# Layer normalisation without affine terms: separate rings for x and y, tiles of 8 rows, and a last store cut into 120 and 8 partitions

## Chip, cores, metric

The kernel runs on one core of one Trainium2 chip. The metric is device time in microseconds; lower is better. The time of a run is some 2 us longer than the span of its profile, which counts from the first to the last instruction.

## The reference

```python
def setup_inputs():
    return {"x": np.random.randn(32, 512, 1024).astype(np.float32), "eps": 1e-5}

def reference(x, eps):
    mean = np.mean(x, axis=-1, keepdims=True)
    var = np.var(x, axis=-1, keepdims=True)
    return ((x - mean) / np.sqrt(var + eps)).astype(np.float32)
```

That is 16384 rows of 1024 floats, 67.11 MB in and 67.11 MB out.

## The kernel before

It takes 4 rows on each of 128 partitions at a time (2 MB), with six buffers for x and six for y. Loads are issued from SP, stores from ACT.

```python
K = 4
xin = ctx.enter_context(tc.tile_pool(name="xin", bufs=6))
yout = ctx.enter_context(tc.tile_pool(name="yout", bufs=6))
st = ctx.enter_context(tc.tile_pool(name="st", bufs=4))
for t in range(ntiles):                                     # 32 tiles
    xt = xin.tile([P, K, D], fdt)
    nc.sync.dma_start(out=xt, in_=x2[rows].rearrange("(p k) d -> p k d", p=P))
    for k in range(K):                                      # DVE: 2 bn_stats and 1 bn_aggr a row
        ...
    # DVE: negmean, vpe = var + eps, ivar = 1 / vpe;  ACT: rstd = sqrt(ivar);  POOL: nmr = negmean * rstd
    ...
    yt = yout.tile([P, K, D], fdt)
    for k in range(K):
        nc.scalar.activation(out=yt[:, k, :], in_=xt[:, k, :], func=AF.Identity,
                             bias=nmr[:, k : k + 1], scale=rstd[:, k : k + 1])
    dst = o2[rows].rearrange("(p k) d -> p k d", p=P)
    nc.scalar.dma_start(out=dst, in_=yt)
```

Of the kernel before, what the change touches and what calls it, by code (L numbers as in the profile page):

```python
# [1 line left out]

# [4 lines left out]


@with_exitstack  # L10
def kernel(
    ctx: ExitStack,
    tc: tile.TileContext,
    x: bass.AP,
    eps: bass.AP,
    out: bass.AP,
):
    nc = tc.nc
    P = nc.NUM_PARTITIONS

    eps_val = float(eps) if not isinstance(eps, bass.AP) else 1e-5

    x2 = x.flatten_outer_dims()
    o2 = out.flatten_outer_dims()
    N, D = x2.shape
    BN_MAX = nc.vector.BN_STATS_FMAX
    assert D % BN_MAX == 0
    NSUB = D // BN_MAX

    K = 4  # L30
    rows_per_tile = P * K
    assert N % rows_per_tile == 0
    ntiles = N // rows_per_tile

    xin = ctx.enter_context(tc.tile_pool(name="xin", bufs=6))
    yout = ctx.enter_context(tc.tile_pool(name="yout", bufs=6))
    st = ctx.enter_context(tc.tile_pool(name="st", bufs=4))

    fdt = mybir.dt.float32
    AF = mybir.ActivationFunctionType  # L40
    ALU = mybir.AluOpType

    for t in range(ntiles):
        rows = slice(t * rows_per_tile, (t + 1) * rows_per_tile)

        xt = xin.tile([P, K, D], fdt)
        nc.sync.dma_start(out=xt, in_=x2[rows].rearrange("(p k) d -> p k d", p=P))  # L47

        stats = st.tile([P, K, NSUB, 6], fdt)
        mv = st.tile([P, K, 2], fdt)  # L50
        for k in range(K):
            for s in range(NSUB):
                nc.vector.bn_stats(  # L53
                    out=stats[:, k, s, :],
                    in_=xt[:, k, s * BN_MAX : (s + 1) * BN_MAX],
                )
            nc.vector.bn_aggr(out=mv[:, k, :], in_=stats[:, k, :, :])  # L57
        negmean = st.tile([P, K], fdt)
        nc.vector.tensor_scalar_mul(out=negmean, in0=mv[:, :, 0], scalar1=-1.0)  # L59
        vpe = st.tile([P, K], fdt)  # L60
        nc.vector.tensor_scalar(  # L61
            out=vpe, in0=mv[:, :, 1], scalar1=eps_val, scalar2=None, op0=ALU.add
        )
        ivar = st.tile([P, K], fdt)
        nc.vector.reciprocal(out=ivar, in_=vpe)  # L65

        rstd = st.tile([P, K], fdt)
        nc.scalar.activation(out=rstd, in_=ivar, func=AF.Sqrt, bias=0.0, scale=1.0)  # L68

        nmr = st.tile([P, K], fdt)  # L70
        nc.gpsimd.tensor_mul(out=nmr, in0=negmean, in1=rstd)  # L71

        yt = yout.tile([P, K, D], fdt)
        for k in range(K):
            nc.scalar.activation(  # L75
                out=yt[:, k, :],
                in_=xt[:, k, :],
                func=AF.Identity,
                bias=nmr[:, k : k + 1],
                scale=rstd[:, k : k + 1],  # L80
            )

        dst = o2[rows].rearrange("(p k) d -> p k d", p=P)
        nc.scalar.dma_start(out=dst, in_=yt)


# [1 line left out]
_INS = ['x', 'eps']  # L88
_OUTS = [((32, 512, 1024), 'float32')]
#: Inputs that are plain numbers.  # L90
_NUMBERS = {'eps': 1e-05}


# [26 lines left out]
```

## Time and profile before

| | before |
|---|---|
| time, median of 3 runs | 321.23 us (321.14 to 321.33) |
| span of the profiled run | 319.0 us |
| busy: DVE, ACT | 181.6 us, 154.3 us |
| bytes, mean rate | 134.27 MB, 421 GB/s |

The page of a profile gives each engine's busy time, then strips of 40 slices of the span. A digit is the busy share of a slice in tenths. In a table of windows each line has: start and end in us, length, the busy us of DVE, ACT and POOL (with their instructions), the clock, the busy share of the 16 DMA engines, and GB/s. A DMA packet is booked in the window in which it starts, so a narrow window can show a share above 1 (2.69 from 314.0 to 314.2 us of this kernel).

### The profile page before, as it was taken

Reading aid. Unit: us, or ns where it says so; the run is one execution under the profiler, and the core shown is the slowest. Engines: PE = TensorE matmul, PEld = TensorE weight load, DVE = VectorE, ACT = ScalarE, POOL = GpSimd, SP = SyncE. Lnnn points to the kernel's source line nnn. Section 1 sums busy time; section 2 is a strip of 40 time slices with the busy share of each in tenths; the row PEclk is TensorE's granted clock in tenths of the full one; section 3 lists DMA queues with packets and bytes.
Section 4 is the critical chain, followed back from the end, with each engine's and each line's share of the span. In section 5 each row is a group of like instructions: output and inputs, shape, how many; then the busy total and the mean of one; then the engine's idle time right before and its main releaser. Section 6 shows DMA issues by size and latency. Waiting matters only on the chain.

```text
span 319.0 us, 926 instructions
## 1 busy us (share of the span) xinstructions
DVE 181.6 (57%) x480; ACT 154.3 (48%) x161; POOL 6.6 (2%) x36
## 2 busy tenths in 40 slices
DVE  0999764457754477544676355765446744467610
ACT  1147491651907419074380833809247091470970
POOL 0000000000000000000000000000000000000000
DMA  7999999999999999999999999999999999999995
GB/s 294 427 405 422 438 431 431 431 429 431 426 429 432 435 431 431 429 427 431 431 433 435 430 431 427 427 431 427 435 438 430 428 431 427 431 427 427 421 427 220
DMA packets 9222, 134.27 MB, mean 421 GB/s; under 512 B 1024, under 2 KB 1024, under 8 KB 1024
## 3 DMA queue, kind: packets, MB, share of 16 engines
q1 hardware_dynamic: 4608, 67.11, 49.6%
q10 hardware_dynamic: 4608, 67.11, 49.2%
q14 instruction: 6, 0.05, 0.0%
HBM read 67.11 MB, written 67.11 MB: 421 GB/s over the span
## 4 chain that ended last, share of the span: by engine, by line
DMA 87%; DVE 4%; issue 3%; ACT 2%; SPq 1%; POOLq 0%; POOL 0%; DVEq 0%
DMA xt<-in_x_dram 87%; DVE stats L53 3%; ACT yt L75 1%; SPq L47 1%; DVE mv L57 0%; DVE ivar L65 0%; DVE negmean L59 0%; POOLq L115 0%; ACT rstd L68 0%; POOL nmr L71 0%; DVE vpe L61 0%; DVEq L65 0%; DVEq L59 0%
## 5 line engine op out<-in xcount | busy, mean ns | idle before, releaser
L53 DVE BATCH_NORM_STATS2 stats<-xt 128x6 f32<-128x512 f32 x256 | 159.4, 665 | 115.3 <-DMA xt<-in_x_dram 115.3
L75 ACT ACTIVATE yt<-xt,nmr,rstd 128x1024 f32<-128x1024 f32 x128 | 146.7, 1227 | 4.7 <-POOL nmr L71 4.5
L68 ACT ACTIVATE rstd<-ivar 128x4 f32<-128x4 f32 x32 | 6.6, 205 | 149.6 <-DVE ivar L65 149.0
L57 DVE BATCH_NORM_AGGREGATE mv<-stats 128x2 f32<-128x12 f32 x128 | 25.1, 196 | 1.1
L71 POOL TENSOR_TENSOR nmr<-negmean,rstd 128x4 f32<-128x4 f32 x32 | 6.3, 198 | 297.9 <-ACT rstd L68 297.9
L65 DVE RECIPROCAL ivar<-vpe 128x4 f32<-128x4 f32 x32 | 5.7, 178 | 3.0
L59 DVE TENSOR_SCALAR negmean<-mv 128x4 f32<-128x4 f32 x32 | 5.4, 170 | 3.1
L61 DVE TENSOR_SCALAR vpe<-mv 128x4 f32<-128x4 f32 x32 | 5.2, 162 | 0.0
L68 ACT ACT_TABLE_LOAD x1 | 1.3, 1283 | 0.7 <-PEq L101 0.7
L101 POOL MEMSET const-float32-0.0<- 128x1 f32 x1 | 0.1, 98 | 0.2 <-issue 0.2
L101 POOL MEMSET const-uint8-127<- 128x1 uint8 x1 | 0.1, 102 | 0.0
L101 POOL MEMSET const-bfloat16-1.0<- 128x1 bf16 x1 | 0.1, 101 | 0.0
L101 POOL MEMSET const-float32-1.0<- 128x1 f32 x1 | 0.1, 98 | 0.0
## 6 DMA issues: line engine op xcount, KB each, us to landing
xt<-in_x_dram SPq DMA_DIRECT2D x32, 2048.0 KB, 38.4
out_dram<-yt ACTq DMA_DIRECT2D x32, 2048.0 KB, 15.5
```

The source lines that it names most:

```text
L47: nc.sync.dma_start(out=xt, in_=x2[rows].rearrange("(p k) d -> p k d", p=P))
L53: nc.vector.bn_stats(out=stats[:, k, s, :], in_=xt[:, k, s * BN_MAX : (s + 1) * BN_MAX],)
L57: nc.vector.bn_aggr(out=mv[:, k, :], in_=stats[:, k, :, :])
L59: nc.vector.tensor_scalar_mul(out=negmean, in0=mv[:, :, 0], scalar1=-1.0)
L61: nc.vector.tensor_scalar(out=vpe, in0=mv[:, :, 1], scalar1=eps_val, scalar2=None, op0=ALU.add)
L65: nc.vector.reciprocal(out=ivar, in_=vpe)
L68: nc.scalar.activation(out=rstd, in_=ivar, func=AF.Sqrt, bias=0.0, scale=1.0)
L71: nc.gpsimd.tensor_mul(out=nmr, in0=negmean, in1=rstd)
L75: nc.scalar.activation(out=yt[:, k, :], in_=xt[:, k, :], func=AF.Identity, bias=nmr[:, k : k + 1], scale=rstd[:, k : k + 1],)
L101: nc = _bacc.Bacc("TRN2", target_bir_lowering=False, num_devices=1)
```

## The change

The intent: larger transfers with fewer packets, the same 48 rows a partition in two rings instead of twelve buffers, small tiles at the end so that little stands after the last load, and a last store that takes work off a DMA engine that is late. The statistics are shortened as well: eps becomes the bias of ACT's square root, and one fused DVE instruction takes the place of the POOL product.

```diff
+TILES = (8, 8, 8, 8, 8, 8, 8, 8, 8, 8, 8, 8, 8, 8, 8, 4, 2, 2)
+XRING = 32
+YRING = 16
+GROUP = 4
+def place(tiles, ring):      # position of each tile in a ring; starts over where a tile does not fit
+    ...
-    xin = ctx.enter_context(tc.tile_pool(name="xin", bufs=6))
-    yout = ctx.enter_context(tc.tile_pool(name="yout", bufs=6))
+    xr = rings.tile([P, XRING, D], fdt)
+    yr = rings.tile([P, YRING, D], fdt)
     ...
-        nc.vector.tensor_scalar_mul(out=negmean, ...)
-        nc.vector.tensor_scalar(out=vpe, ..., op0=ALU.add)
-        nc.vector.reciprocal(out=ivar, in_=vpe)
-        nc.scalar.activation(out=rstd, in_=ivar, func=AF.Sqrt, bias=0.0, scale=1.0)
-        nc.gpsimd.tensor_mul(out=nmr, in0=negmean, in1=rstd)
+        nc.scalar.activation(out=std[:, :G], in_=mv[:, :G, 1], func=AF.Sqrt, bias=eps_t, scale=1.0)
+        nc.vector.reciprocal(out=rstd[:, :G], in_=std[:, :G])
+        nc.vector.scalar_tensor_tensor(out=nmr[:, :G], in0=mv[:, :G, 0], scalar=-1.0,
+                                       in1=rstd[:, :G], op0=ALU.mult, op1=ALU.mult)
     ...
+    with tc.manual_schedule():
+        for (K, row, xp), (_, _, yp) in zip(place(TILES, XRING), place(TILES, YRING)):
+            nc.sync.dma_start(out=xr[:, xp : xp + K, :], in_=rows_of(x2, row, K))
+            for g in range(0, K, GROUP):
+                group(...)                       # statistics and normalisation of up to 4 rows
+            dst, src = rows_of(o2, row, K), yr[:, yp : yp + K, :]
+            cuts = ((0, 120), (120, P)) if (row + K) * P == N else ((0, P),)
+            for a, b in cuts:
+                nc.scalar.dma_start(out=dst[a:b], in_=src[a:b])
```

More of the change, by code (lines that the diff above doesn't have):

```diff
@@ L7 @@
 from concourse._compat import with_exitstack
+TILES = (8, 8, 8, 8, 8, 8, 8, 8, 8, 8, 8, 8, 8, 8, 8, 4, 2, 2)
[3 more added lines that the diff above has]
+def place(tiles, ring):
+    plan, row, pos = [], 0, 0
+    for K in tiles:
+        if pos + K > ring:
+            pos = 0
+        plan.append((K, row, pos))
+        row += K
+        pos += K
+    return plan
 @with_exitstack
@@ L26 @@
     BN_MAX = nc.vector.BN_STATS_FMAX
-    assert D % BN_MAX == 0
     NSUB = D // BN_MAX
-    K = 4
-    rows_per_tile = P * K
-    assert N % rows_per_tile == 0
-    ntiles = N // rows_per_tile
-    xin = ctx.enter_context(tc.tile_pool(name="xin", bufs=6))
-    yout = ctx.enter_context(tc.tile_pool(name="yout", bufs=6))
+    assert sum(TILES) * P == N
+    rings = ctx.enter_context(tc.tile_pool(name="rings", bufs=1))
     st = ctx.enter_context(tc.tile_pool(name="st", bufs=4))
@@ L41, with rows_of, group @@
     ALU = mybir.AluOpType
-    for t in range(ntiles):
-        rows = slice(t * rows_per_tile, (t + 1) * rows_per_tile)
-        xt = xin.tile([P, K, D], fdt)
-        nc.sync.dma_start(out=xt, in_=x2[rows].rearrange("(p k) d -> p k d", p=P))
-        stats = st.tile([P, K, NSUB, 6], fdt)
-        mv = st.tile([P, K, 2], fdt)
-        for k in range(K):
+    xr = rings.tile([P, XRING, D], fdt)
+    yr = rings.tile([P, YRING, D], fdt)
+    eps_t = rings.tile([P, 1], fdt)
+    def rows_of(a, row, K):
+        return a[row * P : (row + K) * P].rearrange("(p k) d -> p k d", p=P)
+    def group(xs, ys, G):
+        stats = st.tile([P, GROUP, NSUB, 6], fdt, name="stats")
+        mv = st.tile([P, GROUP, 2], fdt, name="mv")
+        for k in range(G):
             for s in range(NSUB):
@@ L54 @@
                     out=stats[:, k, s, :],
-                    in_=xt[:, k, s * BN_MAX : (s + 1) * BN_MAX],
+                    in_=xs[:, k, s * BN_MAX : (s + 1) * BN_MAX],
                 )
             nc.vector.bn_aggr(out=mv[:, k, :], in_=stats[:, k, :, :])
-        negmean = st.tile([P, K], fdt)
-        nc.vector.tensor_scalar_mul(out=negmean, in0=mv[:, :, 0], scalar1=-1.0)
-        vpe = st.tile([P, K], fdt)
-        nc.vector.tensor_scalar(
-            out=vpe, in0=mv[:, :, 1], scalar1=eps_val, scalar2=None, op0=ALU.add
-        )
-        ivar = st.tile([P, K], fdt)
-        nc.vector.reciprocal(out=ivar, in_=vpe)
-        rstd = st.tile([P, K], fdt)
-        nc.scalar.activation(out=rstd, in_=ivar, func=AF.Sqrt, bias=0.0, scale=1.0)
-        nmr = st.tile([P, K], fdt)
-        nc.gpsimd.tensor_mul(out=nmr, in0=negmean, in1=rstd)
-        yt = yout.tile([P, K, D], fdt)
-        for k in range(K):
+        std = st.tile([P, GROUP], fdt, name="std")
+        nc.scalar.activation(
+            out=std[:, :G], in_=mv[:, :G, 1], func=AF.Sqrt, bias=eps_t, scale=1.0
+        )
+        rstd = st.tile([P, GROUP], fdt, name="rstd")
+        nc.vector.reciprocal(out=rstd[:, :G], in_=std[:, :G])
+        nmr = st.tile([P, GROUP], fdt, name="nmr")
+        nc.vector.scalar_tensor_tensor(
+            out=nmr[:, :G],
+            in0=mv[:, :G, 0],
+            scalar=-1.0,
+            in1=rstd[:, :G],
+            op0=ALU.mult,
+            op1=ALU.mult,
+        )
+        for k in range(G):
             nc.scalar.activation(
-                out=yt[:, k, :],
-                in_=xt[:, k, :],
+                out=ys[:, k, :],
+                in_=xs[:, k, :],
                 func=AF.Identity,
@@ L81 @@
             )
-        dst = o2[rows].rearrange("(p k) d -> p k d", p=P)
-        nc.scalar.dma_start(out=dst, in_=yt)
+    with tc.manual_schedule():
+        nc.vector.memset(eps_t, eps_val)
+        for (K, row, xp), (_, _, yp) in zip(place(TILES, XRING), place(TILES, YRING)):
+            nc.sync.dma_start(out=xr[:, xp : xp + K, :], in_=rows_of(x2, row, K))
+            for g in range(0, K, GROUP):
+                G = min(GROUP, K - g)
+                a, b = xp + g, yp + g
+                group(xr[:, a : a + G, :], yr[:, b : b + G, :], G)
+            dst, src = rows_of(o2, row, K), yr[:, yp : yp + K, :]
+            cuts = ((0, 120), (120, P)) if (row + K) * P == N else ((0, P),)
+            for a, b in cuts:
+                nc.scalar.dma_start(out=dst[a:b], in_=src[a:b])
 _INS = ['x', 'eps']
```

## The prediction

> **What bounds the kernel now.** I read the page first (busy shares, then the 40 slices, then the queues), then the chain of waits, then windows over the whole span, then very short windows over its last microseconds.
>
> ```profile
> DVE 181.6 (57%) x480; ACT 154.3 (48%) x161; POOL 6.6 (2%) x36
> ...
> DMA  7999999999999999999999999999999999999995
> ...
> q1 hardware_dynamic: 4608, 67.11, 49.6%
> q10 hardware_dynamic: 4608, 67.11, 49.2%
> q14 instruction: 6, 0.05, 0.0%
> ...
> DMA 87%; DVE 4%; issue 3%; ACT 2%; SPq 1%; POOLq 0%; POOL 0%; DVEq 0%
> ```
>
> No compute engine is busy for even 60% of the span, while the DMA engines are at nine tenths or more in every slice but the first and the last. Loads (q1) and stores (q10) took equal shares of the engines for equal bytes. The chain is 87% load transfers. So the transfers are the bound: 67.11 MB in and 67.11 MB out, and the change touches neither figure.
>
> The windows (start:end, length, busy us per engine, clock, DMA share, GB/s) show how little is left:
>
> ```profile
> 0.00:2.00 2.00, 0.00 (x0) 1.27 (x1) 0.20 (x4) 1.00 0.39 74
> 2.00:4.00 2.00, 0.00 (x0) 0.01 (x1) 0.00 (x0) 1.00 0.70 213
> 4.00:14.00 10.00, 5.33 (x13) 0.00 (x0) 0.00 (x0) 1.00 1.01 434
> ...
> 40.00:290.00 250.00, 143.62 (x378) 123.97 (x129) 4.96 (x25) 1.00 1.01 431
> ...
> 315.60:319.00 3.40, 0.00 (x0) 0.00 (x0) 0.00 (x0) 1.00 0.03 14
> ```
>
> At 431 GB/s, 134.27 MB need 311.5 us. By 14 us 0.15 + 0.43 + 4.34 = 4.91 MB have moved, so the DMA behaves as if it had started at 14 - 4.91/0.431 = 2.6 us. The transfers nearly stop at 315.6 us, and 3.4 us of span follow. What is moving there is the finding that the change aims at:
>
> ```profile
> 315.40:315.60 0.20, 0.00 (x0) 0.00 (x0) 0.00 (x0) 1.00 0.19 82
> 315.60:315.80 0.20, 0.00 (x0) 0.00 (x0) 0.00 (x0) 1.00 0.00 0
> ...
> 316.00:316.20 0.20, 0.00 (x0) 0.00 (x0) 0.00 (x0) 1.00 0.19 82
> ...
> 316.60:316.80 0.20, 0.00 (x0) 0.00 (x0) 0.00 (x0) 1.00 0.19 82
> ...
> 317.20:317.40 0.20, 0.00 (x0) 0.00 (x0) 0.00 (x0) 1.00 0.19 82
> ```
>
> 82 GB/s for 0.2 us is 16.4 KB: one packet of 16 KB, one partition's share of a tile. They start 0.6 us apart, and 16 KB in 0.6 us is 27 GB/s, a sixteenth of 431. So a single DMA engine is finishing its partitions alone, until about 317.8 us, while the other fifteen were done near 315.4. The kernel ends some 2.4 us late for one engine.
>
> [...]
>
> **The change part by part.**
>
> *Statistics.* Out go the negated mean, the addition of eps and the POOL product (32 each); in come one fused DVE instruction and the reciprocal per group of up to 4 rows, 15 x 2 + 3 = 33 groups. DVE loses 32 x (170 + 162 + 178 ns) = 16.3 us of instructions and gains 33 x (178 + about 170) = 11.5; busy about 178 us. ACT stays near 154.5, POOL falls to its constants. None of it is on the path: 178 of 319 us is no bound.
>
> *Compute per tile.* A group's statistics take 5.3 us (42.97 to 48.28 in the chain). Sqrt (0.21), reciprocal (0.18), the fused product (0.17) and three handoffs of 0.05 to 0.08 add 0.75, then four normalisations take 4.63 on ACT beside the next group's statistics. A tile of 8 rows costs 2 x 6.05 = 12.1 us in steady state. Its transfers, 2 x 4.19 MB at 431, cost 19.5. Still DMA bound.
>
> *Buffers.* x has 32 rows against 24 now, y 16 against 24. The first store leaves after one load of 8 rows (2.6 + 9.7 + 1.1 = 13.4, the 1.1 being the first landing now, 8.60, minus 2.6 + 4.9), then two groups: 13.4 + 5.3 + 0.75 + 6.05 + 4.63 = 30.1 us, against 19.6 now. Meanwhile loads alone fill the engines; four tiles in the x ring last until 2.6 + 38.9 = 41.5 us, so nothing idles. The first store's bytes start near 32.5, as it must be issued (0.4) and get in behind queued loads (I allow 2). From then on the queues share equally, and loads keep a lead over stores of about (32.5 - 2.6) x 0.431 = 12.9 MB, 3.1 tiles, which fits the rings.
>
> *Packets.* If one partition's 8 rows move as one packet of 32 KB, there are half as many. [...] Semaphore packets per engine fall from 64 to about 37: 0.1 to 0.2 us.
>
> *Last store.* It is 1 MB: 64 KB per engine at 27 GB/s, 2.4 us. If the late engine is the last one, it gets none of it, and its 2.4 us of lateness are just paid off. [...] The extra DMA issue, 0.34 us on ACT, lies beside transfers.
>
> *Sum.* Fifteen engines: 315.4 - 1.1 + 0.3 = 314.6. The late one: 317.8 - 1.1 - 2.4 = 314.3. The end moves from 317.8 to 314.6, -3.2 us: 321.2 - 3.2 = 318.0 us.
>
> **The rivals.** *A hole near the end from the smaller y ring.* Tile 14 (8 rows) may be normalised only once store 12 has landed. From there: 4.63 + 0.75 + 4.63 = 10.1 us of compute, about 1.1 from issue to first byte (the first load's bytes come that long after its issue), and up to 2 for the late engine's part of store 12: 13.2 us. While loads still share the engines store 13 lasts 19.5 us and covers this; with the loads gone it lasts 9.7, and 3.5 us lie idle. With a lead of 3.1 tiles the loads would end just about when store 12 does, so this is a real danger. It would also let the late engine catch up, so the split would bring nothing: 315.4 + 3.5 - 1.1 + 0.3 = 318.1, +0.3: 321.5 us. What speaks against it: the last three loads, of 4, 2 and 2 rows, have packets of 16 and 8 KB beside store packets of up to 32 KB, and get, turn by turn, a third and then a fifth of the engines. 8 rows of loads then stretch from 19.5 us to about 14.6 + 24 = 39, during which stores move 8 + 16 rows, and the loads fill every hole. If packets stay at 16 KB, only the last 4 rows are slowed, and some 2 us of hole remain: about 320.
>
> *The late engine is not the last one, or lateness grows for another reason.* Then the split does nothing: only the 1.1 us of overhead go, 320.1.
>
> *The DVE-ACT round trip or the rings starve the DMA in the middle* (DVE waits for ACT's sqrt in every group, and ACT for a y slot). 12.1 of 19.5 us speaks against it; only a dependency tracked over whole rings would do it, and it would cost tens of us.
>
> *More than 2% faster* needs under 314.8. [...]
>
> **Range and chances.** I give the first sum 60% (318.0), the partly filled hole or the missed engine 25% (320), the full hole 12% (321.5), starvation 2 to 3%. The middle is 318.4; 8 in 10 lie within 316.8 to 321.3. The 2% lines are 314.8 and 327.7: faster 0.03, same 0.95, slower 0.02.
>
> **What would show it.** Right: the middle windows at 431 to 434 GB/s; about 5,200 DMA packets instead of 9,222; the last 15 us at full rate without an idle window; no train of lone 16.4 KB packets after the rest; ACT's first normalisation of a tile waiting for a landed store in the middle, harmlessly. Wrong: a window near 290 to 300 us with no bytes, with ACT waiting for an output transfer before it (the y ring); a lone late engine still there (the split missed); some 9,000 packets (no larger ones, no gain in rate); slices under 9 in the middle (starvation).

Its sum came to 318.0 us, 3.2 less than before:

- Packets, 1.1 us off for every engine. 1.0 of it was the estimate of what half as many packets are worth. The rest is for the semaphore packets: the records have 64 packets of 4 bytes per engine before and 36 after, of 9 ns each: 28 fewer are 0.25 us.
- Last store, 2.4 us off for the late engine and 0.3 on for others. The author took the part of 120 partitions to leave one engine out ("the last one" in the text), supposed that this is the late one, and took the part of 8 to give some of the others a ninth packet of 8 KB, 0.3 us. One engine left out and one with a ninth packet are in the records of the changed kernel (below). That the one left out is the late one they do not show: it ended at 312.1 us, the latest at 318.7.

The sum for "more than 2% faster": at the measured 431 GB/s it is 311.5 + 2.6 before the transfers + 1.2 after the last packet + 2.2 beyond the span, 317.5 us: still not under 314.8.

## The result

| | before | after |
|---|---|---|
| time, median of 4 runs | 321.28 us (321.14 to 321.36) | 321.80 us (321.31 to 323.10) |
| span of the profiled run | 319.0 us | 320.1 us |
| busy: DVE, ACT | 181.6, 154.3 us | 186.9, 158.1 us |
| DMA packets | 9222 | 5197 |

The ratio is 1.0023, with a 95% interval of 1.0003 to 1.0043: no gain, and a trace of a loss. (A ratio is the mean time of one kernel's fast runs over that of the other's of the same rounds, so it is not quite the ratio of the medians.) One of the four runs of the changed kernel, 323.10 us, stands apart from the other three. The main sum had forecast 3.2 us of gain; the medians show 0.5 us of loss.

From the page of the changed kernel, the strip, the rates and the queues:

```profile
DMA  8999999999999999999999999999999999999994
...
DMA packets 5197, 134.27 MB, mean 419 GB/s; under 512 B 583, under 2 KB 583, under 8 KB 583
...
q14 instruction: 6, 0.05, 0.0%
```

The packets are fewer, 3840 of them of 32 KB, so one partition's 8 rows do move as one packet, and the transfers are still the bound: nine tenths or more in all slices but the ends. As before, six packets are instruction fetches (q14); keep them in mind.

From the waits of the changed kernel, and its windows over the middle and the end:

```profile
ACT yr L90 <- DMA out_dram<-yr: 106.9, 14, 10.4
```

```profile
100.00:200.00 100.00, 60.15 (x145) 50.74 (x53) 0.00 (x0) 1.00 1.01 433
200.00:290.00 90.00, 55.82 (x136) 46.32 (x49) 0.00 (x0) 1.00 1.00 430
...
310.00:312.00 2.00, 0.00 (x0) 0.00 (x0) 0.00 (x0) 1.00 0.98 397
312.00:314.00 2.00, 0.00 (x0) 0.00 (x0) 0.00 (x0) 1.00 0.99 279
314.00:316.00 2.00, 0.00 (x0) 0.00 (x0) 0.00 (x0) 1.00 0.79 250
316.00:318.50 2.50, 0.00 (x0) 0.00 (x0) 0.00 (x0) 1.00 0.22 85
```

ACT now waits 107 us for stores to free slots of the small y ring, and in the middle that costs nothing: 430 to 433 GB/s, as the 431 before. The new thing is at the end. From 312 to 314 us the DMA engines are busy (0.99) but move only 279 GB/s, so each packet takes longer than its size explains. That is the last store, the one that was cut. After it comes a thin tail up to 318.5 us.

The packet records of the trace carry no engine number, but each packet starts where another of its engine ended, so they can be strung into 16 chains (in the kernel before, 511 to 517 packets of 8 or 16 KB each; a sixteenth of all is 512). In the changed kernel one chain ends at 312.1 us and has nothing of the last store: that is the engine left out, and it was one of the first to be done. The two chains that end last, at 318.3 and 318.7 us, each have the full eight packets of the last store, and the latest has a ninth as well, from the part of 8 partitions. The slow packets, of up to 1.28 us instead of 0.31, are on other engines: the latest chain, followed back packet by packet, runs at 0.31 us without a gap through its last two stores, so it was late before the last store began. So the cut relieved an engine that was early and loaded the late one.

### The profile page after: what moved, and what is told of

The parts are those of the page before. It is cut to its first block, busy times and chain, and to the rows that moved or that the text cites. A ratio compares the mean times of both kernels' runs of the same rounds, so it can differ in the third digit from the quotient of the medians.

```text
span 320.1 us, 730 instructions
## 1 busy us (share of the span) xinstructions
DVE 186.9 (58%) x451; ACT 158.1 (49%) x162; POOL 0.2 (0%) x4
## 2 busy tenths in 40 slices
DMA packets 5197, 134.27 MB, mean 419 GB/s; under 512 B 583, under 2 KB 583, under 8 KB 583
## 4 chain that ended last, share of the span: by engine, by line
DMA 64%; ACT 22%; DVE 9%; issue 1%; another core or an unknown queue 0%; ACTq 0%
DMA out_dram<-yr 60%; ACT yr L90 21%; DVE stats L68 7%; DMA xr<-in_x_dram 4%; DVE mv L72 1%; ACT std L75 1%; DVE rstd L79 1%; DVE nmr L81 1%; ACTq L110 0%; ACTq L90 0%
## 5 line engine op out<-in xcount | busy, mean ns | idle before, releaser
L90 ACT ACTIVATE yr<-xr,nmr,rstd 128x1024 f32<-128x1024 f32 x128 | 148.4, 1229 | 115.2 <-DMA out_dram<-yr 106.9
L68 DVE BATCH_NORM_STATS2 stats<-xr 128x6 f32<-128x512 f32 x256 | 159.2, 664 | 12.8 <-DMA xr<-in_x_dram 12.8
L79 DVE RECIPROCAL rstd<-std 128x4 f32<-128x4 f32 (+1 forms) x33 | 5.9, 178 | 100.7 <-ACT std L75 100.7
L72 DVE BATCH_NORM_AGGREGATE mv<-stats 128x2 f32<-128x12 f32 x128 | 26.7, 209 | 4.4
L75 ACT ACTIVATE std<-mv,eps_t 128x4 f32<-128x4 f32 (+1 forms) x33 | 9.6, 292 | 35.1 <-DVE mv L72 34.6
L81 DVE SCALAR_TENSOR_TENSOR nmr<-mv,rstd 128x4 f32<-128x4 f32 (+1 forms) x33 | 5.4, 162 | 1.1
## 6 DMA issues: line engine op xcount, KB each, us to landing
xr<-in_x_dram SPq DMA_DIRECT2D x15, 4096.0 KB, 46.2
xr<-in_x_dram SPq DMA_DIRECT2D x2, 1024.0 KB, 61.8
out_dram<-yr ACTq DMA_DIRECT2D x1, 1024.0 KB, 11.5
```

The source lines that it names most:

```text
L68: nc.vector.bn_stats(out=stats[:, k, s, :], in_=xs[:, k, s * BN_MAX : (s + 1) * BN_MAX],)
L72: nc.vector.bn_aggr(out=mv[:, k, :], in_=stats[:, k, :, :])
L75: nc.scalar.activation(out=std[:, :G], in_=mv[:, :G, 1], func=AF.Sqrt, bias=eps_t, scale=1.0)
L79: nc.vector.reciprocal(out=rstd[:, :G], in_=std[:, :G])
L81: nc.vector.scalar_tensor_tensor(out=nmr[:, :G], in0=mv[:, :G, 0], scalar=-1.0, in1=rstd[:, :G], op0=ALU.mult, op1=ALU.mult,)
L90: nc.scalar.activation(out=ys[:, k, :], in_=xs[:, k, :], func=AF.Identity, bias=nmr[:, k : k + 1], scale=rstd[:, k : k + 1],)
```

## The experiments

**Theories.** S: the cut of the last store itself costs time, since it relieves the wrong engine and makes the packets slow. Y: the small y ring ate the gain (the rival of the prediction). I: an engine is late because it also fetches instructions. Y2: that ring leaves a hole near the end, where small tiles do not fill it. L and N, defined where they are tested: why a cut store is slow.

### One undivided last store (a_one_store)

```diff
-            cuts = ((0, 120), (120, P)) if (row + K) * P == N else ((0, P),)
+            cuts = ((0, P),)
```

> The changed kernel with its last store of 2 rows undivided. Theory S (the split itself costs: the engine that it leaves out was early, [...]and the 120-partition store runs its packets of 8 KB at half speed in places): the end comes 0.8 to 1.5 us sooner, 320.3 to 321.0 us, and the last 3 us before the lone packets run at over 400 GB/s. Rival Y (the small y ring is what ate the gain): within 0.3 us of the changed kernel, 321.5 to 322.1. Rival of the prediction (the late engine is the last one and the split did help): 2 us later, 324.

Measured: 321.28, 323.71, 320.51, 323.63, 320.24 and 323.31 us, a ratio to before of 1.0027 (0.9993 to 1.0062). The runs fall into two groups, and the mean hides that. The group of the profiled run is about 1 us faster than the three runs of the changed kernel near 321.6, which is what S expected. The other is 2 us slower, which nobody expected. In the profile of the fast group the slow packets are gone, though not the tail of late engines (windows of this run):

```profile
312.00:314.00 2.00, 0.00 (x0) 0.00 (x0) 0.00 (x0) 1.00 0.94 393
314.00:316.00 2.00, 0.00 (x0) 0.00 (x0) 0.00 (x0) 1.00 0.52 217
316.00:318.00 2.00, 0.00 (x0) 0.00 (x0) 0.00 (x0) 1.00 0.12 49
```

393 GB/s where the cut had 279. On the time this run is inconclusive.

### The cut alone, in the kernel before (b_before_split)

```diff
-        nc.scalar.dma_start(out=dst, in_=yt)
+        cuts = ((0, 120), (120, P)) if t == ntiles - 1 else ((0, P),)
+        for c, d in cuts:
+            nc.scalar.dma_start(out=dst[c:d], in_=yt[c:d])
```

> The kernel before with only its last store (4 rows, packets of 16 KB) cut into 120 and 8 partitions. Theory S: one more packet of 0.6 us on the late engine and slowed packets: 322 to 324 us. Prediction's theory (the late engine is the last one, and is left out of eight packets of 0.6 us): some 2.5 us sooner, 318.5 to 319. Rival Y says nothing of this run.

Measured: 324.27 us, ratio 1.0100 (1.0087 to 1.0113), some 3.1 us slower. The same windows over the last store, first of this run, then of the kernel before:

```profile
310.00:316.00 6.00, 0.00 (x0) 0.00 (x0) 0.00 (x0) 1.00 0.86 235
316.00:320.00 4.00, 0.00 (x0) 0.00 (x0) 0.00 (x0) 1.00 0.62 156
```

```profile
310.00:316.00 6.00, 0.00 (x0) 0.00 (x0) 0.00 (x0) 1.00 0.84 358
316.00:318.00 2.00, 0.00 (x0) 0.00 (x0) 0.00 (x0) 1.00 0.06 25
```

The same bytes at 235 instead of 358 GB/s, with the engines as busy: in the records many of the 16 KB packets took about 1.2 us instead of 0.61. The prediction's mechanism would have made this run some 2.5 us faster. S holds here.

### Rings of 24 and 24, one undivided store (c_rings24)

```diff
-XRING = 32
-YRING = 16
+XRING = 24
+YRING = 24
 (and the undivided last store, as in a_one_store)
```

> The changed kernel with one undivided last store and both rings of 24 rows (three tiles of 8 each). Theory S: the waits for y slots go, but the transfers were never starved by them, so within 0.4 us of the run with one store. Rival Y: at least 1.5 us sooner than that run.

Measured: 320.92 us (320.78 to 321.04), ratio 0.9990 (0.9978 to 1.0002). The scatter of a_one_store is gone, so the comparison with its mixed median says little; against its fast group the time is the same within 0.4 us. Y, which wanted 1.5 us, is not supported, though the new end of this run blurs the comparison. What sets the end is something else (timeline and windows of this run):

```profile
308.10 1.29 DVE L68 BATCH_NORM_STATS2 stats<-xr 128x6 f32<-128x512 f32 x2 [8.47 <-DMA xr<-in_x_dram]
```

```profile
312.00:315.00 3.00, 0.00 (x0) 2.15 (x2) 0.00 (x0) 1.00 0.06 25
315.00:317.00 2.00, 0.00 (x0) 0.00 (x0) 0.00 (x0) 1.00 1.05 434
```

DVE waited 8.5 us for the last load, whose packets are of 8 KB where the stores have 16 and 32 KB. What that does was counted in the records of the changed kernel. In its chains a packet of one queue is followed by one of the other in 88% of the cases between 60 and 260 us, where all are of 32 KB. Unequal packets take turns as well (91% and 93%), so small ones get less: from 266 to 278 us 100 load packets, nearly all of 16 KB, started beside 109 store packets of 32 KB and had 31% of the bytes; from 284 to 290 us 55 of 8 KB beside 64 of 32 KB had 18%. That is near the third and the fifth of the prediction. In this run the load came too late: the last tile was computed after everything else had been stored, in a hole of 3 us, in which the late engine caught up.

### The same rings with the cut kept (j_rings24_split)

```diff
-            cuts = ((0, P),)
+            cuts = ((0, 120), (120, P)) if (row + K) * P == N else ((0, P),)
```

> The changed kernel with rings of 24 and 24 and its cut last store kept; beside the run with rings of 24 and one undivided store (320.9, five runs within 0.3 us, where a hole of 3 us before the last store had let the late engine catch up) it differs in the cut alone. Theory S (a store of 120 partitions runs many packets at half speed, and no late engine is there to be helped): the last store takes 4 to 5 us instead of 2.6, 322 to 323.5 us. Rival (the cut costs nothing once the late engine has caught up): 320.6 to 321.2.

Measured: 323.14 us (323.05 to 323.74), ratio to before 1.0065, where the run without the cut had 0.9990; the two medians are 2.2 us apart. The hole and all before it are the same, so this is the cleanest measure of the cut:

```profile
312.00:315.00 3.00, 0.00 (x0) 2.16 (x2) 0.00 (x0) 1.00 0.06 25
315.00:317.00 2.00, 0.00 (x0) 0.00 (x0) 0.00 (x0) 1.00 1.07 229
```

229 GB/s against 434 in the same window at the same busy share. S is shown: the cut slows its own store by about half, late engine or not.

### What makes it slow: 96 and 32 partitions (g_cut96)

```diff
+        cuts = ((0, 96), (96, P)) if t == ntiles - 1 else ((0, P),)   # in the kernel before
```

> The kernel before with its last store (4 rows) cut into 96 and 32 partitions[...]. The cut into 120 and 8 cost 3 us there, with packets of 16 KB that took 1.2 us instead of 0.61. Theory L[...]: slow as well, 322.5 to 325 us, with windows of 200 to 300 GB/s after 310 us. Rival N (the slowness comes from using 15 engines and leaving one out): within 0.5 us of before.

Measured: 321.69 us, ratio 1.0015 (1.0002 to 1.0029). Theory L had every store cut by partitions slow; N had only one that leaves an engine out slow. Neither expectation fits. The time is N's, but the windows show slow packets here too:

```profile
310.00:316.00 6.00, 0.00 (x0) 0.00 (x0) 0.00 (x0) 1.00 0.99 320
316.00:318.00 2.00, 0.00 (x0) 0.00 (x0) 0.00 (x0) 1.00 0.40 139
```

So leaving an engine out is not needed to make the packets slow; a cut by partitions was enough in both runs, with more or less effect (320 and 235 GB/s from 310 to 316 us, where the whole store had 358). What makes the packets of a cut store take longer was not shown. Why 96 and 32 cost only 0.4 us can be read from the packet chains. In the kernel before, fifteen end at 315.3 to 316.0 us and the late one at 317.9; here all sixteen end between 316.3 and 318.3, so none was left out. So the slow packets cost most engines 1 to 2 us or more, and nearly all of that is hidden behind the lateness that was there before. With 120 and 8 the last engines end at 321.0, too late to be hidden. Why that cut is the slower of the two stays open.

### The transfers alone (d_copy)

Stores straight from the x ring, no compute. Its output is wrong, which doesn't matter for the time.

```diff
-            for g in range(0, K, GROUP):
-                ...
-            dst, src = rows_of(o2, row, K), yr[:, yp : yp + K, :]
+            dst, src = rows_of(o2, row, K), xr[:, xp : xp + K, :]
 (and the undivided last store)
```

> Wrong on purpose: the same loads and stores (undivided last store), stores straight from the x ring, no statistics and no normalisation. It asks what the transfers alone take and whether one engine is late without the instruction stream of the compute. If the late engine comes from fetching instructions (six 8 KB fetches in the profile before), there is no train of lone packets at the end and the time is 317 to 319 us; if it comes from the engine itself, the train stays and the time is 319.5 to 321.5.

Measured: 317.78 us (317.30 to 318.85), ratio 0.9895. The windows of its end:

```profile
312.00:314.00 2.00, 0.00 (x0) 0.00 (x0) 1.00 0.98 406
314.00:315.00 1.00, 0.00 (x0) 0.00 (x0) 1.00 0.34 139
315.00:316.00 1.00, 0.00 (x0) 0.00 (x0) 1.00 0.00 0
```

All sixteen engines are done by 314.7 us, with no tail of lone packets. (There is no ACT column, as ACT computes nothing.) This run has no instruction fetch in its span. Nearly the same bytes, and no engine is late: in this case lateness does not come from the engine itself.

### The transfers with idle instructions (e_copy_instr)

```diff
+            for _ in range(100):
+                nc.vector.memset(eps_t, eps_val)        # in d_copy, for each of the 18 tiles
```

> Wrong on purpose, as the copy without compute, with 1800 tiny memsets added on DVE that no transfer waits for. Theory I (an engine is late because it also fetches the instructions, 8 KB at a time, about 0.31 us each): some 14 fetches more in the instruction queue, and if they fall on one DMA engine it is 4 us late: 321 to 322.5 us with a train of lone packets at the end; if they fall on several engines, less. Rival (lateness comes from the loads and stores of the full kernel contending with its compute): as the copy, 317.3 to 318.3, no train.

Measured: 330.08 us, ratio 1.0276, 12.3 us slower than the copy, and three times what was expected. Its queues and windows:

```profile
q14 instruction: 14, 0.11, 0.1%
```

```profile
290.00:300.00 10.00, 0.00 (x0) 0.00 (x0) 1.00 0.85 361
300.00:310.00 10.00, 0.00 (x0) 0.00 (x0) 1.00 0.55 238
310.00:316.00 6.00, 0.00 (x0) 0.00 (x0) 1.00 0.85 360
316.00:319.00 3.00, 0.00 (x0) 0.00 (x0) 1.00 0.08 36
```

14 fetches of 8 KB at 0.31 us are 4.4 us of DMA time, a third of what was lost. The packet records have the rest. The packet that starts when a fetch ends took 1.69 to 1.89 us in all 14 cases, where 1.21 is usual for 32 KB: 8.8 us more. Together that is 13.2 us of extra work, and the run is 12.3 us slower, as if one engine had nearly all of it. At the end one engine does stand alone: between 319.7 and 322.5 us the remaining load packets follow one another singly. The other fifteen wait for this one (238 GB/s at a busy share of 0.55 from 300 to 310). Theory I holds, with a fetch that costs its engine about three times its own length, the slow packet included.

The kernel before shows the same. After 25.5 us just six of its 7603 packets of 16 KB took more than 0.69 us, and they are the six that follow a fetch (1.14, 0.85, 1.22, 0.95, 0.85 and 1.23 us instead of 0.61). The steps can also be read from the landings in its trace:

```
fetches (us):                             29.5   83.3  101.4  179.5  239.4  248.9
last engine after the last but one,
loads landing at (us):      62: 1.1   101: 1.1   122: 2.0   170: 1.7   181: 2.7   249: 2.2   259: 3.1
```

The lag of loads steps up after three of the fetches (101.4, 179.5, 248.9), to 2.0, 2.7 and 3.1 us, and it shrinks a little between them; after those at 83.3 and 239.4 it does not. The packet chains tell why: with the compute in place, the fetches fall on two engines. In i_halves (below), where every chain comes out with its full number of packets, four of the six fetches lie on the engine that ends last, and the two others on the one that ends last but one. Which engine's instructions each of them fetches was not asked.

### Which engine is late (p8, p4, p1)

Extra loads in the kernel before, into a scratch tile, in tiles 6 to 9; the first number of partitions is 8, then 4, then 1.

```diff
+        if t in (6, 7, 8, 9):
+            a = t - 6
+            nc.sync.dma_start(out=xe[a : 32 : 4],          # p4: a : 16 : 4, p1: a : 4 : 4
+                              in_=x2[rows].rearrange(...)[a : 32 : 4, 0:3])
```

No trace gives an engine its number, so the numbers are cut from the three expectations. What each of them came to: 1.4 to 2.2 us slower than before (1.5 to 2.1 in p1) if the late engine is among those that its extra loads run on, and within 0.4 us of before if it is not. The 1.8 us are four packets of 12 KB on one engine, 48 KB at its 27 GB/s.

> The kernel before with four small extra loads into a scratch tile early on (tiles 6 to 9): 8 partitions each, four apart, 12 KB a partition. [...] Others were done about 2.4 us before the late engine in the kernel before, so extra work of 1.8 us shows only where the late engine gets it. Theory S[...]: 1.4 to 2.2 us slower than before, 322.7 to 323.5. Rival[...]: within 0.4 us of before.

> The same with 4 partitions in each of the four extra loads[...]: 1.4 to 2.2 us slower than before.[...]

> The kernel before with the four extra loads of one partition each (12 KB)[...]. 8 and 4 partitions both cost 1.7 to 1.9 us[...].

Measured: 323.16 us with 8 (ratio 1.0062), 322.97 with 4 (1.0055), 321.20 with 1 (1.0001). So the late engine is among those that the loads of 4 partitions run on. In p4's records the four extra packets of tile 6 started at 51.15, 51.23, 51.36 and 52.67 us, which fits one of four engines being already 1.3 us behind. In p1 each extra load is a single packet of 12 KB, so it ran on one engine; whether on the same one each time was not shown. The runs only show that the loads of 4 partitions delay the late engine and those of one partition do not. The mechanism was not quite the expected one: the added 1.8 us show less as a longer tail than as a hole (windows of p4, then of before):

```profile
294.00:298.00 4.00, 1.92 (x8) 1.50 (x3) 0.20 (x1) 1.00 0.64 274
```

```profile
294.00:298.00 4.00, 0.35 (x3) 3.21 (x4) 0.20 (x1) 1.00 0.99 418
```

A late engine that gets later makes the others wait (274 instead of 418 GB/s), as in e_copy_instr.

### Tiles of one size, rings of 24 (f_rings24_8s)

```diff
-TILES = (8, 8, 8, 8, 8, 8, 8, 8, 8, 8, 8, 8, 8, 8, 8, 4, 2, 2)
+TILES = (8,) * 16
 (in c_rings24)
```

> The changed kernel with rings of 24 rows each, sixteen tiles of 8 rows and one undivided last store. The run with rings of 24 had a hole of 3 us near the end, while it waited for the last loads in their small packets; with tiles of one size the loads share evenly to the end and the hole should go, but the late engine then stands at the end again. Theory: 319.6 to 320.4 us, with no empty window and a train of lone packets of 32 KB. Rival (large last tile: its compute and store stand alone at the end): a hole before the last store, 322 to 326 us.

Measured: 319.90 us (319.85 to 320.04), ratio 0.9959 (0.9947 to 0.9972). This beats both kernels. The 3 us hole is gone, yet a small one is left, and with it a short tail:

```profile
300.00:305.00 5.00, 0.34 (x2) 4.56 (x5) 0.00 (x0) 1.00 0.78 334
305.00:310.00 5.00, 0.00 (x0) 0.17 (x1) 0.00 (x0) 1.00 0.98 419
310.00:315.00 5.00, 0.00 (x0) 0.00 (x0) 0.00 (x0) 1.00 0.97 419
315.00:318.30 3.30, 0.00 (x0) 0.00 (x0) 0.00 (x0) 1.00 0.03 10
```

In the chains fifteen engines end at 315.8 to 315.9 us and one at 317.0. No window is empty, as expected, but 334 GB/s for 5 us are about 1.1 us lost.

### Filling that hole (i_halves)

```diff
+                if (row + K) * P == N:             # last tile: store each half (4 rows) when it is ready
+                    nc.scalar.dma_start(out=rows_of(o2, row, K)[:, g : g + G], in_=yr[:, b : b + G, :])
+            if (row + K) * P < N:
+                nc.scalar.dma_start(out=rows_of(o2, row, K), in_=yr[:, yp : yp + K, :])
```

> The run with rings of 24 and sixteen tiles of 8, with the last tile stored in two halves of 4 rows (128 partitions each), each as soon as its group is normalised. In that run the transfers fell to 334 GB/s from 300 to 305 us, a hole of about 1.1 us, and one engine ended 1.2 us after the rest. If the late engine sets the end, filling the hole only makes it stand 2.4 us after the rest: within 0.4 us of 319.9. If the hole set the end: about 1.1 us sooner, 318.8.

Measured: 320.07 us (319.93 to 320.21), ratio 0.9964. No gain, as the theory of the late engine wanted:

```profile
300.00:305.00 5.00, 0.30 (x2) 4.63 (x4) 0.00 (x0) 1.00 0.96 415
...
314.00:317.00 3.00, 0.00 (x0) 0.00 (x0) 0.00 (x0) 1.00 0.06 27
```

The hole is filled (415 GB/s), fourteen engines are done by 314.2 us, one at 314.6, and one moves 27 GB/s, a sixteenth of 431, until 316.9. The first of these two late ones has two fetches in its chain (95.7, 303.2 us), the last has four (37.5, 118.2, 203.9, 294.3). A gain for fifteen engines of sixteen is no gain. The run also answers a rival of theory S: here the last tile goes out as two stores, both of 128 partitions, and their packets keep 0.61 us for 16 KB. So two stores in place of one are not slow by themselves; the cut by partitions is.

### The same tiles, rings of 32 and 16 (h_8s)

```diff
-XRING = 24
-YRING = 24
+XRING = 32
+YRING = 16
 (in f_rings24_8s)
```

> The changed kernel (rings of 32 and 16) with sixteen tiles of 8 rows and one undivided last store; beside the run with sixteen such tiles and rings of 24 and 24 (319.9) it differs in the rings alone. Theory Y2 (the hole that the prediction feared: the y ring of two tiles makes tile 14 wait for store 12, and 10 us of compute and 3 of latency stand against 9.7 us of store 13): an empty or half-empty stretch of 2 to 4 us near 295 to 300, 320.5 to 323 us. Rival: rings do not matter, 319.6 to 320.3.

Measured: 324.34 us (324.10 to 326.70), ratio 1.0096; 4.4 us slower than with rings of 24. The profiled execution is the slowest of the five, 326.70 us, so its hole is larger than that of the others. Its timeline of ACT and its windows:

```profile
290.37 4.63 ACT L90 ACTIVATE yr<-xr,nmr,rstd 128x1024 f32<-128x1024 f32 x4 [7.30 <-DMA out_dram<-yr]
...
300.30 0.34 ACTq L110 DMA_DIRECT2D out_dram<-yr  x1
```

```profile
296.00:300.00 4.00, 3.90 (x10) 4.00 (x4) 0.00 (x0) 1.00 0.12 51
```

ACT waits for a store until 290.4, computes 8 rows, and issues the next store 9.9 us later, while the engines run dry from 296. Between 294 and 302 us about 5 us of full rate are missing (213 GB/s for 2 us, 51 for 4, 262 for 2, against 431). This is the prediction's first rival, which had been put at 3.5 us. The changed kernel, with the same rings, has no such hole (424 GB/s from 290 to 300 us, 401 from 300 to 310). It differs in its small tiles at the end, whose slow loads (two of 1 MB took 61.8 us from issue to landing, those of 4 MB 46.2), as the prediction argued, fill it.

### Two more looks at the scatter (a2_one_store, a3_one_store)

The kernel is that of a_one_store, unchanged.

> A repeat of the changed kernel with one undivided store, for its profile: its six runs fell into two groups, 320.2 to 321.3 and 323.3 to 323.7 us, and the profile was of the first. If this one is of the second group, theory Y2 expects an empty stretch of some 3 us between 290 and 310 us that the first profile has not; the rival is slow packets in the middle with no empty stretch.

> The same again, as the group cannot be chosen. Same expectation.

Measured: 320.83 and 320.61 us, one run each: both of the fast group, so no profile of the slow group was caught. With rings of 24 the runs of a kernel lay within 0.7 us of each other; with 32 and 16 all three kernels spread over 1.8 us or more (the changed kernel, a_one_store, h_8s). Why is open.

## Why the prediction was wrong

**The step that failed** is the part "Last store": "If the late engine is the last one, it gets none of it, and its 2.4 us of lateness are just paid off." The late engine is another. It kept its eight packets of the last store (2.4 us) and got a ninth (0.3). The sum put its end at 314.3; it came at 318.7. Of these 4.4 us, 2.7 are the last store. Of the rest, 1.1 are the saving of the next item, which the sum had taken off and this engine's end does not show, and 0.6 stay open. That the store of 120 partitions would be slow as a whole was not in the sum at all: the cut cost 2.2 us with rings of 24, where no engine was late any more, and 3.1 in the kernel before. The rival "the late engine is not the last one" had been named, but priced as if the cut were then harmless ("the split does nothing"). It does harm.

**The packet saving was mis-sized for this kernel.** 1.1 us were forecast. By the packet records the changed kernel is 0.34 MB ahead of before at 280 us, 0.8 us at 431 GB/s, and 0.21 MB, 0.5 us, at 310 us. c_rings24, which differs up to there in the rings alone, is 0.30 MB (0.7 us) ahead at 280 and 0.48 MB (1.1 us) at 310. So the size is about right in the middle, and with rings of 32 and 16 part of it was lost again between 280 and 310 us.

**The lateness was taken as given, and as a property of an engine's number.** That was the assumption; no trace shows it. Here the copy has no late engine (all are done by 314.7 us), and 14 fetches make one very late (12.3 us).

**What was right.** The transfers are the bound and keep 431 GB/s or so in the middle; packets of 32 KB (5197 against the 5,200 foretold); the compute of a tile lies beside its transfers; the y ring's hole, which h_8s shows when the small tiles are taken away; the unequal turns of small packets beside large ones (18 to 31% of the bytes for the loads). ACT's wait for y slots in the middle is harmless, as foretold.

**Wrong without effect.** DVE's busy time rose to 186.9 us, where 178 was forecast. The forecast took instruction times from busy time, but these overlap (in the kernel before they add up to 200.8 us, in 181.6 us of busy time). ACT came to 158.1 us instead of 154.5, as its square root with the bias took 292 ns on average instead of 205. Neither is on the path. One sum is slightly off: 181.6 - 16.3 + 11.5 is 176.8, not 178; no conclusion hangs on it.

**Open:** the slow group of a_one_store; why the packets of a cut store take longer; why the packet after a fetch is slow; the exact number of the late engine.

## What to carry to other kernels

When the DMA engines are the bound, the end is set by the latest of sixteen (here 2.4 us after the rest): look for a tail of lone packets before tuning buffers, and find out which engine it is (small extra transfers on a few engines) before moving work. Store all 128 partitions at once, and cut by rows if you must cut; a cut into 120 and 8 partitions halved the rate of its own store (229 GB/s instead of 434), while two halves of 4 rows kept 0.61 us for a packet of 16 KB. Instructions are transfers too: here 1800 unrolled instructions brought 14 fetches of 8 KB and made one engine late, by more than the fetches' own length (12.3 us, where the fetches take 4.4), and every transfer waited for that one.
